# Even attention of a two-block transformer kernel: TensorE's order written out by steps of the heads

## The chip, the cores and the metric

The kernel runs on one core of one Trainium2 chip. A core has five engines that this text speaks of: TensorE (PE, matrix products, with its weight loads as PEld), VectorE (DVE), ScalarE (ACT), GpSimd (POOL) and SyncE (SP, which issues the loads). Each works through its own instructions in the order in which they stand; they wait for one another by semaphores. The metric is the device time of one execution in microseconds (us).

## The reference

Two blocks work on 512 tokens of 1024 features and on a context of 256 tokens. Block 0 ("even") mixes by a gated MLP over chunks and a differential attention; block 1 ("odd") by windowed attention; each is followed by a gated feed-forward part. The change lies in the even attention and the products beside it. Cut to that:

```python
u, v, q, k, vv = jnp.split(h @ w_in, [A_WIDTH, 2 * A_WIDTH, KV_START, KV_START + B_QK_WIDTH], axis=-1)
q = apply_rope(q.reshape(b, s_len, 2 * B_HEADS, HEAD_DIM), cos, sin)
k = apply_rope(k.reshape(b, s_len, 2 * B_HEADS, HEAD_DIM), cos, sin)
...
def diff_attn(q, k, v, lam):          # 4 heads, each a pair of 64-wide softmaxes
    s = jnp.einsum('bqhd,bkhd->bhqk', q, k).astype(jnp.float32) * ATTN_SCALE
    p = jax.nn.softmax(s, axis=-1).reshape(b, B_HEADS, 2, tq, tk)
    a = p[:, :, 0] - lam * p[:, :, 1]
    return jnp.einsum('bhqk,bkhe->bqhe', a.astype(v.dtype), v)
...
def chunk_mlp(u, v, w_s, b_s):        # u and v through Gelu, v normalised over 128 features,
    ...                               # mixed by a 128x128 matrix per group, times u
y = jnp.concatenate([chunk_mlp(u, v, w_s, b_s), diff_out(o, subln_g, lam_init)], axis=-1) @ w_out
```

`diff_out` is an RMS norm over a head's 128 features. The context goes through the same mixer with its own queries and keys.

## The kernel before

All activations lie transposed, features on the 128 partitions and the 768 tokens (512 and 256 of context) along the row. Products are taken in three passes with operands split into a high and a low part (`mm3`, lines 103 to 108: high x high, high x low, low x high). `split` (L122, L123) makes the parts: a cast on ScalarE, a subtraction on VectorE. Weights come by `blocks` and `unit`: a load, a cast on ScalarE (L81), a subtraction on GpSimd (L84).

In `even`, after the values are there (tiles `vhi`, `vlo`), three things are done side by side up to the output projection:

- The attention. There are four heads `t`, each with three pairs `qp` of blocks of 128 queries; pair 2 is the context's and sees 256 keys only. `stack_q` and `stack_k` lay a head's q and k out on the partitions as high and low halves (`qa`, `qb`, `kh`, `kl`). `softmax_diff` takes two score products (`c` = 0, 1) into `wide()` banks (tile `pw`, two of them), their maxima on VectorE (L538), their exponentials on ScalarE (L540, tile `e`), and the weighted difference on VectorE (L546). `attend` transposes the result in groups of four on TensorE (L558, into a `bank()`, tile `pb`, three of them), splits it (`ath`, `atl`) and multiplies by the values into `o`. `norm` squares `o`, sums on TensorE (L156), makes a reciprocal root in small VectorE instructions and spreads it (L183).
- Twelve filling products of 128 output features each, in a `fill()` bank (tile `pf`, a single one): four for q and k of heads 2 and 3 (`qk1`), eight for u and v (`gated`, tiles `raw`). Each is 24 instructions for the 512 tokens and 24 for the context, each followed by an evacuation on ScalarE (L445, L579).
- Gelu of the fillers (L626, another ScalarE table than Exp's), the transposes and statistics of the gate (`turn`, L638 to L643), and later its normalisation (L653, L655) and mixing (`mix`, L656).

What sets the order: the kernel is built with a scheduler that, per engine, takes the ready instruction of highest priority, and writes the order down; a chip follows that order. Heads 0 and 1 have a higher priority than the q/k fillers, heads 2 and 3 a higher one than the v fillers, and `issue_after` puts an instruction behind a named one in the scheduler's eyes. Heads 2 and 3 stand behind the last of the Gelus of the four v tiles:

```python
        for i in (4, 5, 6, 7):
            last = gelu(i, self.last_exp)
        with tc.high_priority(offset=tc.cur_priority - here), tc.issue_after(last.ins):
            head(2)
            head(3)
```

## Time and profile before

| what | us |
|---|---|
| median of 3 runs (1587.4 to 1593.12) | 1588.67 |
| the profiled execution, its own time | 1590.09 |
| its span in the profile | 1588.3 |
| TensorE busy, share of the span | 1517.7, 96% |
| VectorE busy | 1090.5, 69% |
| ScalarE busy | 723.5, 46% |
| GpSimd busy | 830.8, 52% |

The mean granted TensorE clock is 0.988 of full speed. A row of the order of time reads: start, duration, engine, line, operation, tile written <- tiles read, shapes, count; in brackets the idle time of the engine just before it and what ended that. "x4" merges four instructions that follow one another. The even attention and its fillers lie from about 129.5 us to 336 us, the output projection behind that.

### The profile page before, as it was taken

The page shows a single profiled execution, that of the slowest core. Times are in us where ns is not written, and L with a number is a line of the kernel's source. Part 1 is how long each engine was busy: PE and PEld are TensorE (multiplying, and loading weights), DVE is VectorE, ACT ScalarE, POOL GpSimd, SP SyncE. Part 2 cuts the span into 40 slices and gives each one's busy share as a digit, 9 for nine tenths or more (in the row PEclk, how much of TensorE's full clock was granted, in tenths as well). Part 3 has the DMA queues.
Part 4 walks back from the last instruction along what each step waited for, and adds up shares of the span by engine and source line. Part 5 has one row for each costly group of instructions (what it writes and reads, how often), then busy time and mean ns, then how long its engine had stood idle before and what let it go on. Part 6 is the DMA issues. An engine that isn't in the chain of part 4 may idle for free.

```text
span 1588.3 us, 24991 instructions
## 1 busy us (share of the span) xinstructions
PE 1517.7 (96%) x9547; PEld 1352.1 (85%) x9547; DVE 1090.5 (69%) x1958; ACT 723.5 (46%) x1472; POOL 830.8 (52%) x565
## 2 busy tenths in 40 slices
PE   6999997999999999999999989999999999999996
PEld 4767886889999999999999978777869989999996
DVE  3617847775697787888785485666667976666656
ACT  2415656553553333333333244565655644444443
POOL 0453321060347776777676415541304398888883
PEclk9999998999999999999999999999999999999998
DMA  9771010033223333444452122110225132323301
GB/s 353 290 253 60 28 33 1 1 133 133 67 74 120 113 109 118 139 163 141 162 169 63 27 66 67 60 34 12 70 80 206 54 120 87 113 91 109 93 14 54
DMA packets 54295, 162.00 MB, mean 102 GB/s; under 512 B 6176, under 2 KB 10656, under 8 KB 46496
## 3 DMA queue, kind: packets, MB, share of 16 engines
q1 hardware_dynamic: 47120, 135.11, 25.5%
q10 hardware_dynamic: 7056, 25.30, 4.9%
q8 instruction: 75, 1.23, 0.3%
q14 instruction: 44, 0.36, 0.1%
HBM read 158.29 MB, written 2.10 MB: 101 GB/s over the span
## 4 chain that ended last, share of the span: by engine, by line
PE 72%; DVE 8%; ACT 3%; issue 1%; POOL 0%; POOLq 0%; ACTq 0%; DVEq 0%
PE pw L108 10%; PE pw L106 10%; PE pw L107 10%; PE pb L108 8%; PE pb L107 8%; PE pb L106 8%; PE pf L106 3%; PE pf L107 3%; PE pf L108 3%; PE pb L1432 2%; PE pb L1421 2%; PE pw L1384 1%; PE pw L1392 1%; DVE t L884 1%; DVE T L123 1%
## 5 line engine op out<-in xcount | busy, mean ns | idle before, releaser
L84 POOL TENSOR_TENSOR w<-raw,w 128x512 fp32r<-128x512 f32 (+1 forms) x86 | 129.6, 1513 | 255.0 <-ACT w L81 232.7
L779 DVE SCALAR_TENSOR_TENSOR xT<-pb,mod,xT 128x512 f32<-128x512 f32 (+3 forms) x208 | 145.8, 707 | 125.9 <-PE pb L108 125.7
L106 PE MATMUL pw<-ax,w 128*128 128x384 f32 (+2 forms) x708 | 223.5, 319 | 4.1 <-DVE q L884 1.9
L107 PE MATMUL pw<-ax,w 128*128 128x384 f32 (+2 forms) x708 | 224.3, 318 | 2.7 <-DVE ax L465 1.4
L108 PE MATMUL pw<-ax,w 128*128 128x384 f32 (+2 forms) x708 | 223.7, 317 | 0.1
L884 POOL TENSOR_TENSOR w<-raw,w 128x512 fp32r<-128x512 f32 x110 | 169.0, 1552 | 19.7 <-ACT w L884 19.5
L884 POOL TENSOR_TENSOR w<-t,w 128x512 fp32r<-128x512 f32 x99 | 149.6, 1514 | 55.6 <-ACT w L884 55.6
L106 PE MATMUL pf<-ax,w 128*128 128x256 f32 (+2 forms) x484 | 163.2, 337 | 10.9 <-DVE qf L252 6.3
L106 PE MATMUL pb<-hh,w 128*128 128x512 f32 x480 | 171.0, 356 | 1.2 <-DVE xT L779 1.2
L108 PE MATMUL pb<-hh,w 128*128 128x512 f32 x480 | 171.5, 357 | 0.3 <-DVE w L884 0.3
L107 PE MATMUL pb<-hh,w 128*128 128x512 f32 x480 | 171.1, 356 | 0.0
L108 PE MATMUL pf<-ax,w 128*128 128x256 f32 (+2 forms) x484 | 161.1, 333 | 0.0
L107 PE MATMUL pf<-ax,w 128*128 128x256 f32 (+2 forms) x484 | 160.4, 331 | 0.0
L107 PE MATMUL pw<-T,w 128*128 128x384 f32 (+1 forms) x508 | 157.0, 310 | 1.2 <-DVE T L123 1.2
L106 PE MATMUL pw<-T,w 128*128 128x384 f32 (+1 forms) x508 | 156.3, 310 | 1.1 <-DVE hs L884 1.1
L108 PE MATMUL pw<-T,w 128*128 128x384 f32 (+1 forms) x508 | 157.0, 310 | 0.0
L106 PEld LDWEIGHTS pw<-ax,w 128*128 128x128 f32 x708 | 134.0, 190 | 9.7 <-DVE q L884 2.6
L107 PEld LDWEIGHTS pw<-ax,w 128*128 128x128 f32 x708 | 134.7, 190 | 8.4 <-DVE ax L201 2.4
L108 PEld LDWEIGHTS pw<-ax,w 128*128 128x128 f32 x708 | 134.6, 190 | 2.1 <-DVE w L953 0.4
L884 POOL TENSOR_TENSOR hh<-hs,hh 128x768 fp32r<-128x768 f32 (+1 forms) x42 | 80.2, 1910 | 90.1 <-ACT hh L884 67.6
L884 POOL TENSOR_TENSOR w<-rawo,w 128x512 fp32r<-128x512 f32 x59 | 103.6, 1756 | 28.3 <-ACT w L884 28.3
L106 PEld LDWEIGHTS pf<-ax,w 128*128 128x128 f32 x484 | 92.4, 191 | 19.6 <-DVE qf L252 3.8
(379 smaller groups left out, 3924.1 us busy)
## 6 DMA issues: line engine op xcount, KB each, us to landing
raw<-ffn_in SPq DMA_DIRECT2D x44, 1024.0 KB, 5.3
ar<-ada SPq DMA_DIRECT2D x24, 1024.0 KB, 7.1
ar<-ada ACTq DMA_DIRECT2D x48, 512.0 KB, 3.6
rawo<-ffn_out SPq DMA_DIRECT2D x88, 256.0 KB, 3.0
raw<-odd_out SPq DMA_DIRECT2D x32, 256.0 KB, 2.7
raw<-qk SPq DMA_DIRECT2D x16, 256.0 KB, 6.5
raw<-uv SPq DMA_DIRECT2D x16, 256.0 KB, 2.7
raw<-even_out SPq DMA_DIRECT2D x8, 512.0 KB, 3.6
```

What stands on the lines that cost most here:

```text
L84: eng.tensor_tensor(lo, raw, hi.bitcast(F32), ALU.subtract)
L106: mm(out, s[0], m[0], start=start, stop=False, **kw)
L107: mm(out, s[0], m[1], start=False, stop=False, **kw)
L108: return mm(out, s[1], m[0], start=False, stop=stop, **kw)
L123: return (lo_eng or nc.vector).tensor_tensor(lo, src, hi.bitcast(F32), ALU.subtract)
L779: ins = self.nc.vector.scalar_tensor_tensor(h, ps[:, r], self.modcol(l, j, m, who), h, ALU.mult, ALU.add)
L884: tail[key] = fn(*args, **kw)
L1384: nc.tensor.matmul(ps[:, st:en], Q, K[g][p][:, b0 * P:b1 * P], start=p == 0, stop=p == 1, skip_group_check=True)
L1392: nc.tensor.matmul(ps[:, en:en + TC], Q, K[g][p][:, TX:], start=p == 0 and not edge, stop=p == 1, skip_group_check=True)
L1421: last = nc.tensor.transpose(pt[:, x * P:(x + 1) * P], es[2 * (x % 2) + x // 2][:, kb * P:(kb + 1) * P], self.ident)
L1432: nc.tensor.matmul(po[64 * h:64 * h + 64, :], V[vb][:, 64 * g:64 * g + 64], t[:, h * TC:h * TC + TC], start=kb == 0, stop=kb == nb - 1, sk ...
```

## The change

The heads' functions are cut into steps, and every TensorE instruction of this part is put behind the one before it (`pe`, `tail`), so TensorE's order is the one written. There are 13 steps: step `n` does the scores of pair `n` and, in between, the transposes and value products of pair `n - 1`, by one of two plans. After each item `fill_in` takes pieces (six instructions: two of the eight k blocks) from one queue of all fillers, so many that their estimated time keeps up with 1.5 times (later 1.15 times) that of the attention. `stack` is made per half of a head (`c`), each with its own tile, all subtractions on VectorE (head 3's were GpSimd's); the transposes of `turn` go to `bank()` and stand in steps 9 to 11; the four Gelus of the v tiles come at the end of step 8.

```diff
+        def pe(fn, *args):
+            with tc.issue_after(tail[0].ins) if tail else ExitStack():
+                tail[:] = [fn(*args)]
...
+        def stack(t, c):
+            X, Y = (slice(0, 64), slice(64, 128))[::(1, -1)[c]]
...
+            nc.scalar.copy(m[X], q[X])
...
+            nc.scalar.copy(kh[X], k[X])
+            nc.scalar.copy(kh[Y], k[X])
+            nc.vector.tensor_tensor(m[Y], q[X], m[X].bitcast(F32), ALU.subtract)
+            for Z in (X, Y):
+                nc.vector.tensor_tensor(kl[Z], k[X], kh[X].bitcast(F32), ALU.subtract)
...
+        def block(name, n, out, scale, done=None):
...
+            for c, A, us in ((slice(0, TX), axx, 1.38), (slice(TX, TA), axc, 0.72)):
+                box = []
+                def step(k0, c=c, A=A, box=box):
+                    if k0 == 0:
+                        box.append(self.fill()[:, :c.stop - c.start])
+                    pe(piece, box[0], A, k0)
+                    if k0 == KT - 2:
+                        nc.scalar.mul(u[:, c], box[0], scale)
+                        if done and c.start:
+                            done(u)
...
-        here = tc.cur_priority
-        for n, key in enumerate((2, 6, 3, 7)):
-            W = self.blocks(a["qk1"][n])
...
-        with tc.high_priority(offset=tc.cur_priority - here):
-            QK = {0: stack(0)}
-            for t in range(2):
-                head(t)
...
-        for g in range(4):
-            turn(g)
-            gated(g, after if g == 3 else None)
+        share = (1.5, 1.15)
...
+        def fill_in(us):
+            clock[0] += us * share[n > 8]
+            while queue and clock[1] < clock[0]:
+                f, d, fn = queue.pop(0)
+                ahead(f + 3)
+                fn()
+                clock[1] += d
+        ahead(2)
+        stack(0, 0)
+        stack(0, 1)
...
+            long = prev and prev["qp"] < 2
+            plan = "00 01 t0 t1 a0 t2 10 11 a1 a2" if long else "00 t0 a0 01 10 11"
+            for v in plan.split():
+                if v[0] in "ta":
+                    if prev:
+                        (turned if v[0] == "t" else weighed)(prev, int(v[1]))
+                        fill_in(0.35 if v[0] == "t" else 0.71)
+                elif cur:
+                    i, c = int(v[0]), int(v[1])
+                    with tc.issue_after(last_gelu.ins) if last_gelu else ExitStack():
+                        scores(t, 2 * qp + i, c, cur["b"][i])
+                    fill_in(0.7 if qp < 2 else 0.24)
...
+                if t and qp < 2:
+                    norm(t - 1, 1 + qp)
+                    fill_in(1.2 - 0.5 * qp)
+                if n == 8:
+                    while queue[0][0] < 8:
+                        fill_in(0.5)
+                    for i in (4, 5, 6, 7):
+                        last_gelu = gelu(i, self.last_exp)
+                    fill_in(3.0)
+                if n >= 9:
+                    for g in ((0, 1), (2,), (3,))[n - 9]:
+                        turn(g)
+            prev = cur
+        fill_in(3.0)
+        norm(3, 1)
+        fill_in(100.0)
+        norm(3, 2)
```

In a plan, "00" is a score product (block, `c`), "t0" a group of transposes, "a0" the product with the values. The order of the built programs at three places (a number behind a tile's name is its own; `ax` and `w` are activations and weights of a filler, `pw` a score bank).

TensorE behind the last product ahead of the attention, before: 21 rows of the first filler like the first three stand ahead of these.

```order
L106 MATMUL pf_1065<-ax_328,w_1061 128x512
L107 MATMUL pf_1065<-ax_329,w_1061 128x512
L108 MATMUL pf_1065<-ax_328,w_1061 128x512
L536 MATMUL pw_1348<-kh_1332,qa_1326 128x512
L537 MATMUL pw_1348<-kh_1332,qa_1326 128x256
L536 MATMUL pw_1348<-kl_1333,qa_1326 128x512
L537 MATMUL pw_1348<-kl_1333,qa_1326 128x256
L536 MATMUL pw_1356<-kh_1338,qb_1327 128x512
L537 MATMUL pw_1356<-kh_1338,qb_1327 128x256
```

TensorE at the same place, changed; `t_997` belongs to the product ahead.

```order
L371 MATMUL pb_996<-ident_103,t_997 128x128 x4
L559 MATMUL pw_1106<-kh_1088,qa_1086 128x512
L560 MATMUL pw_1106<-kh_1088,qa_1086 128x256
L559 MATMUL pw_1106<-kl_1089,qa_1086 128x512
L560 MATMUL pw_1106<-kl_1089,qa_1086 128x256
L106 MATMUL pf_1126<-ax_314,w_1068 128x512
L107 MATMUL pf_1126<-ax_315,w_1068 128x512
L108 MATMUL pf_1126<-ax_314,w_1068 128x512
L106 MATMUL pf_1126<-ax_316,w_1068 128x512
L107 MATMUL pf_1126<-ax_317,w_1068 128x512
L108 MATMUL pf_1126<-ax_316,w_1068 128x512
```

The filler's 512 tokens stood whole ahead of the first score product; now that product comes first and a piece of six stands between it and the next.

VectorE at the same place, before (`qa_1532` and `kl_1539` are head 1's, `f_160` the first filler):

```order
L265 TENSOR_TENSOR qb_1327<-f_56_330,qb_1327 64x768
L279 TENSOR_TENSOR kl_1333<-f_57_331,kh_1332 64x768 x2
L265 TENSOR_TENSOR qa_1532<-f_58_332,qa_1532 64x768
L279 TENSOR_TENSOR kl_1339<-f_57_331,kh_1338 64x768 x2
L279 TENSOR_TENSOR kl_1539<-f_59_333,kh_1538 64x768 x2
L538 TENSOR_REDUCE sa_1346<-pw_1348 128x1
L251 STREAM_SHUFFLE sh_1117<-f_160_1064 128x512
L538 TENSOR_REDUCE sa_1346<-pw_1356 128x1
```

VectorE changed (`qa_1348` and `kl_1351` are head 1's):

```order
L546 TENSOR_TENSOR kl_1089<-f_57_331,kh_1088 64x768 x2
L544 TENSOR_TENSOR qa_1095<-f_56_330,qa_1095 64x768
L544 TENSOR_TENSOR qa_1348<-f_58_332,qa_1348 64x768
L546 TENSOR_TENSOR kl_1098<-f_57_331,kh_1097 64x768 x2
L567 TENSOR_REDUCE sa_1111<-pw_1106 128x1
L546 TENSOR_TENSOR kl_1351<-f_59_333,kh_1350 64x768 x2
L567 TENSOR_REDUCE sa_1111<-pw_1133 128x1
L579 SCALAR_TENSOR_TENSOR sx_1104<-sa_1112 128x1
L575 RECIPROCAL sa_1141<-sa_1112 128x1
```

The first maximum (of `pw_1106`) moved ahead of head 1's `kl`; the second stands behind that.

ScalarE at the end of the attention, before (`o_2463` is head 3's, `pf_3070` and `pf_3096` the two parts of the last filler):

```order
L570 COPY o_2463<-pb_2726 128x256
L595 ACTIVATE sq_2743<-o_2463 128x768
L653 ACTIVATE f_357_1917<-f_357_1917,sf_3161,sf_3149 128x128 x3
L653 ACTIVATE f_364_1980<-f_364_1980,sf_3161,sf_3149 128x128 x3
L653 ACTIVATE f_371_2043<-f_371_2043,sf_3161,sf_3149 128x128 x3
L653 ACTIVATE f_378_2106<-f_378_2106,sf_3161,sf_3149 128x128 x3
L579 COPY f_585_3069<-pf_3070 128x512
L122 CAST ax_3227<-o_1344 128x768
```

ScalarE changed (`pf_2966` is the context's part of the last filler but one, `pf_3033` the first part of the last):

```order
L122 CAST ath_3000<-pb_2995 128x512
L616 COPY o_2505<-pb_3004 128x256
L657 ACTIVATE sq_3024<-o_2505 128x768
L703 ACTIVATE f_160_1058<-f_160_1058,sf_3161,sf_3149 128x128 x3
L703 ACTIVATE f_161_1059<-f_161_1059,sf_3161,sf_3149 128x128 x3
L703 ACTIVATE f_162_1060<-f_162_1060,sf_3161,sf_3149 128x128 x3
L703 ACTIVATE f_163_1061<-f_163_1061,sf_3161,sf_3149 128x128 x3
L641 ACTIVATE f_166_1064<-pf_2966 128x256
L674 ACTIVATE f_166_1064<-f_166_1064 128x768
L641 ACTIVATE f_167_1065<-pf_3033 128x512
```

The twelve normalisations stood ahead of the evacuation of the last filler's first part; now they stand ahead of that of the last part of the filler before it, with a Gelu behind.

More of the change, by code (lines that the diff above doesn't have):

```diff
@@ L562, in attend @@
-                self.split(th, tl, pt)
+                        ins = nc.tensor.transpose(pt[:, j * TC + b * P:j * TC + (b + 1) * P],
+                                                  pair["b"][b]["e"][0][:, (2 * i + j) * P:(2 * i + j + 1) * P], self.ident)
+                return ins
+            pe(products)
+            th = Ra.tile([P, 512], F32R, name=self.uid("ath"), tag="at", bufs=6)
+            tl = Ra.tile([P, 512], F32R, name=self.uid("atl"), tag="at", bufs=6)
+            self.split(th, tl, pt)
@@ L635, in turn @@
             for off, n in halves:
[L636 to L638 removed]
+                ps = self.bank()
+                with tc.issue_after(tail[0].ins):
+                    for i in range(n):
+                        ins = nc.tensor.transpose(ps[:, i * P:(i + 1) * P], vg[:, (off + i) * P:(off + i + 1) * P], self.ident)
+                tail[:] = [ins]
                 nc.scalar.copy(vg[:, off * P:(off + n) * P], ps[:, :n * P])
@@ new lines, in even, with ahead @@
+        fillers = [block("qk1", n, (key, qk), 0.125 if key < 4 else 1.0, turn_em) for n, key in enumerate((2, 6, 3, 7))]
+        fillers += [block("uv", i, (i, raw), 1.0) for i in (4, 5, 6, 7, 0, 1, 2, 3)]
+        loads = [f[0] for f in fillers]
+        queue = [(n, us, fn) for n, f in enumerate(fillers) for us, fn in f[1]]
+        clock = [0.0, 0.0]
+        share = (1.5, 1.15)
+        def ahead(n):
+            while loads and len(fillers) - len(loads) < n:
+                loads.pop(0)()
```

170 lines of the change are left out of this document (86 added, 84 removed).

## The prediction

> **What bounds the kernel now.** I read the page first (busy shares, chain), then the stretches of the even attention, then the rows of its holes.
>
> ```profile
> span 1588.3 us, 24991 instructions
> PE 1517.7 (96%) x9547; PEld 1352.1 (85%) x9547; DVE 1090.5 (69%) x1958; ACT 723.5 (46%) x1472; POOL 830.8 (52%) x565
> PE 72%; DVE 8%; ACT 3%; issue 1%; POOL 0%; POOLq 0%; ACTq 0%; DVEq 0%
> ```
>
> TensorE (PE) is the bound: the kernel can only gain where TensorE stands still, and loses wherever it is made to. Columns of the next view: stretch, its length, busy time (instructions) of PE, weight loads, VectorE (DVE), ScalarE (ACT), GpSimd (POOL), then TensorE's granted clock, DMA share and GB/s.
>
> ```profile
> 130.00:155.00 25.00, 23.28 (x131) 19.80 (x131) 23.16 (x33) 15.35 (x26) 10.68 (x8) 1.00 0.11 33
> 155.00:190.00 35.00, 32.95 (x205) 29.02 (x204) 30.01 (x53) 21.90 (x45) 12.55 (x9) 1.00 0.15 46
> 190.00:235.00 45.00, 43.67 (x276) 38.72 (x275) 25.15 (x57) 25.27 (x49) 8.72 (x6) 1.00 0.10 30
> 235.00:260.00 25.00, 17.40 (x77) 13.80 (x76) 13.50 (x33) 13.82 (x25) 4.35 (x3) 0.73 0.00 1
> 260.00:330.00 70.00, 64.15 (x416) 55.45 (x415) 54.76 (x187) 42.65 (x93) 4.80 (x4) 1.00 0.11 38
> sum 200.00, PE 181.45 PEld 156.79 DVE 146.57 ACT 118.98 POOL 41.10; mean PE 36.29 PEld 31.36 DVE 29.31 ACT 23.80 POOL 8.22
> ```
>
> These 200 us are what the change rewrites. TensorE idles 200 - 181.45 = 18.6 us in them. VectorE is busy 146.6 us, and in the first 25 us 93%: early on it is nearly a second bound. The one large hole:
>
> ```profile
> 234.53 0.39 PE L106 MATMUL pf<-ax,w 128*128 128x256 f32 x1 [0.89 <-ACT f L579]
> ...
> 241.69 0.50 PE L536 MATMUL pw<-kh,qa 128*128 128x512 f32 x1 [2.91 <-ACT e L540]
> ...
> 247.06 0.47 PE L558 MATMUL pb<-ident,e 128*128 128x128 f32 x1 [2.87 <-DVE e L546]
> ...
> 253.75 0.63 PE L107 MATMUL pf<-ax,w 128*128 128x512 f32 x1
> ...
> 257.00 0.39 PE L107 MATMUL pf<-ax,w 128*128 128x512 f32 x1
> ```
> ```profile
> 238.49 0.85 ACT L626 ACTIVATE f<-f 128x768 f32<-128x768 f32 x1
> 239.35 1.28 ACT L540 ACT_TABLE_LOAD   x1
> 240.64 0.90 ACT L540 ACTIVATE e<-pw,sa 128x768 f32<-128x768 f32 x1
> ```
>
> Four filler products had to be finished before their Gelus, the Gelus before the table goes back to Exp, and head 2 behind that; nothing was left to fill with. TensorE's clock fell to half: the same product took 0.63 us at 253.75 and 0.39 at 257.00. A mean clock of 0.73 over 25 us is 13.5 us at half rate, two thirds of it busy, so about 4.5 us lost. One gap more: a product's modelled end lies 0.16 us behind the next one's start (0.39 long, 0.23 apart, rows below), so each of some 24 gaps hides 0.16 us: 3.6. With a few waits too short to be listed, before loses 18.6 + 4.5 + 3.6 + 2 = 29 us here (27 to 30). The products are the same in both kernels, so the forecast is the loss of the new order against this 29.
>
> **The change, part by part.** I walk the new order row by row with durations of this profile. First its start.
>
> ```profile
> 129.50 0.48 PE L106 MATMUL pf<-ax,w 128*128 128x512 f32 x1
> 129.81 0.40 PE L107 MATMUL pf<-ax,w 128*128 128x512 f32 x1
> 130.04 0.39 PE L108 MATMUL pf<-ax,w 128*128 128x512 f32 x1
> ...
> 135.04 0.39 PE L536 MATMUL pw<-kh,qa 128*128 128x512 f32 x1
> ...
> 135.74 0.39 PE L536 MATMUL pw<-kh,qb 128*128 128x512 f32 x1
> ```
> ```profile
> 128.93 0.84 ACT L261 ACTIVATE qa<-f 64x768 fp32r<-64x768 f32 x1
> ...
> 130.66 0.83 ACT L276 CAST kh<-f 64x768 fp32r<-64x768 f32 x1
> ...
> 139.96 0.90 ACT L540 ACTIVATE e<-pw,sa 128x768 f32<-128x768 f32 x1 [0.25 <-DVE sa L538]
> ```
> ```profile
> 130.07 0.95 DVE L265 TENSOR_TENSOR qa<-f,qa 64x768 fp32r<-64x768 f32 x1
> ...
> 132.28 1.91 DVE L279 TENSOR_TENSOR kl<-f,kh 64x768 fp32r<-64x768 f32 x2
> ...
> 138.97 0.96 DVE L538 TENSOR_REDUCE sa<-pw 128x1 f32<-128x768 f32 x1
> ...
> 145.34 1.02 DVE L546 SCALAR_TENSOR_TENSOR e<-e,sa,e 128x768 f32<-128x768 f32 x1
> ...
> 148.91 0.74 DVE L251 STREAM_SHUFFLE sh<-f 128x512 f32<-128x512 f32 x1
> 149.68 0.69 DVE L252 TENSOR_TENSOR f<-f,cos 128x512 f32<-128x512 f32 x1
> ```
>
> A score product takes 135.74 - 135.04 = 0.70 us, a piece of a filler six times 0.23 = 1.4 us (0.7 for the context's 256 columns). *Step 0.* Before, TensorE fills from 129.50 while the stacks are made. Now its next row is the first score product: kh is there at 131.5, kl (VectorE: qa 0.95, kl 1.9) at 133.2, score done at 133.7; one piece, 135.0. The second score's kl stands on VectorE behind two qa's, one for the next head: 133.2 + 4 x 0.95 = 137.0, done 137.4; piece, 138.7. The third wants the bank of the first: maximum (0.96, behind that kl) 137.9, exponential (0.90) 138.9, done 139.7; piece. The fourth wants the second's bank, whose maximum stands behind the next head's kl (1.9): 140.7, exponential 141.6, done 142.5; piece, 143.8. That is 4 x 0.70 + 4 x 1.4 = 8.3 us of work in 14.3: **6.0 lost**. *Step 1.* The same queue delays two scores by 2.0 us; the first transposes need the sum of weights (1.02) that stands behind shuffle, rope product (0.74, 0.69) and two maxima: 151.4, when TensorE is there at 148.6; then the split of the transposes 0.75 late and an evacuation 0.75: **6.3 lost**. Together 12, where before idles 1.7 us up to 155 (25.00 - 23.28).
>
> ```profile
> 327.62 0.39 PE L106 MATMUL pf<-ax,w 128*128 128x256 f32 x1 [1.44 <-ACT f L579]
> ...
> 332.06 1.16 PE L656 MATMUL pf<-sguT,f 128*128 128x128 f32 x8
> ...
> 336.14 0.42 PE L106 MATMUL pw<-ax,w 128*128 128x384 f32 x1
> ```
>
> *Steps 2 and 3*, walked alike: the stacks of two heads (six VectorE instructions of 0.95) stand ahead of a maximum: 2.6; the rest 1.1: **3.7**. *Steps 4 to 8.* All fillers share one PSUM bank. In three places the order puts a new tile's first piece right behind the old tile's last: the wait is 0.89 (row above, ScalarE free) to 1.44 (at 327.62, ScalarE busy), 1.15 taken as the middle: 3.5; three more are half covered, 1.5; weighed products too close behind their transposes, 0.9; VectorE and ScalarE queues 2: **8** (4 to 11).
>
> ```profile
> 309.98 0.59 ACT L122 CAST ath<-pb 128x512 fp32r<-128x512 f32 x1 [0.44 <-PE pb L558]
> ```
> ```profile
> 310.60 0.69 DVE L123 TENSOR_TENSOR atl<-pb,ath 128x512 fp32r<-128x512 f32 x1 [0.33 <-ACT ath L122]
> ```
>
> From a transpose group's start to its low half are 0.6 + 0.6 + 0.7 + 0.2 for hand-overs = 2.1 us; where the order puts less between, TensorE waits for the rest.
>
> *The Gelus (step 8).* Load 1.28 and three Gelus at 0.85 stand on ScalarE ahead of the evacuation that the next filler tile needs: 3.1; the second load ahead of nothing urgent; a split 0.9: **4.2**, against 13 in the hole. *Steps 9 to 11.* Four transpose groups of the gate want three banks, and their 12 statistics (with 12 aggregates) stand on VectorE ahead of the weights' splits: 3.5; others 2.3: **5.8**.
>
> ```profile
> 322.36 4.73 ACT L653 ACTIVATE f<-f,sf,sf 128x128 f32<-128x128 f32 x12 [2.01 <-DVE sf L704]
> 327.01 0.56 ACT L579 COPY f<-pf 128x512 f32<-128x512 f32 x1
> ```
> ```profile
> 319.39 0.18 DVE L135 TENSOR_SCALAR sf<-sf 128x24 int32<-128x24 int32 x1
> ...
> 321.71 0.18 DVE L139 SCALAR_TENSOR_TENSOR sf<-sf,sf 128x24 f32<-128x24 f32 x1
> ```
>
> *The last step.* A table load and two Gelus (3.0) stand ahead of a filler's evacuation: 2.3 after cover. The last transposes have nothing between them and their product: 2.2. Then ScalarE's order has the twelve normalisations (4.73 in one run, and behind VectorE's chain of small instructions, 321.71 + 0.18 - 319.39 = 2.5) ahead of the evacuation of the last but one filler, and TensorE's order has only that filler's next tile: TensorE done at 12.5 of this step, evacuation done at 17.8: **5.3**. Before pays 1.44 there, since the filler ahead of it was long. One more uncovered tile, 1.1. Sum **10.8**; the half clock may add 0 to 2.
>
> *The end.* From the last tile's start to the projection are 336.14 - 327.62 = 8.5 us; with the gate's normalisation done earlier it is four pieces of 0.7, about 1.4 of spread norms and 1.3 of gate products (1.16 for four in the row at 332.06, and two more), 5.5; less some 1 for the gate products now deferred: **2 gained**. GpSimd's stack of head 3 goes to VectorE (1.9 us, inside the walk). The loads of filler weights keep their order, two blocks ahead: nothing.
>
> Sum: 6.0 + 6.3 + 3.7 + 8 + 4.2 + 5.8 + 10.8 = 45 lost against 29, less 2: +14 us. The profiled execution's span is 1588.3; the runs' median is 1588.67, so 1588.7 + 14 = **1603 us** (0.9% slower).
>
> [...]
>
> **The rivals.** (a) *The same, 1588:* VectorE keeps nearer to TensorE than my walk has it (its rows overlap by some 0.08 us each, which I only partly count). Then steps 1 to 3 and 9 to 11 lose some 4 instead of 16, and 1603 - 12 = 1591, with the ends a little less 1588. For it: VectorE is busy 147 of 200 us only. Against: the first 25 us at 93%. It decides at the first transposes of step 1: a wait under 1 us is this case. (b) *Faster, 1574:* the pieces cover the chain of maximum, exponential and sum (about 4 us) everywhere after step 1, and only the start (6), the Gelus (4) and the last step (6) stay: 16 - 29 - 2 = -15. For it: 4 to 8 us of work lie between a step's last score and the transposes that need it. Against: single waits on one bank and on splits, which no sharing removes. It decides where steps 2 to 8 lose under 2 us in all. (c) *Slower still, 1608:* the clock halves at the start (busy under half in 129 to 139) and at the stall of 5.3, as it did behind the 2.91 us gap; a spell of 4 us at half rate costs 2 to 3, twice. [...]
>
> **How the numbers follow.** Main 0.41 (1596 to 1606), (c) 0.20, (a) 0.24, (b) 0.15. A difference under 0.5% (8 us) is about what this measurement can't tell from none, so faster 0.15, same 0.24, slower 0.61. The range leaves out (b) and the upper tail: 1581 to 1613; the likeliest case alone is 1596 to 1613.
>
> **What would show it.** Right: no half clock in the middle; TensorE waits at the first scores (5 to 6 us in all before 144); a wait of 2 to 3 us before step 1's transposes; one of about 5 us behind the last but one filler, released by ScalarE's evacuation; waits of fillers on their bank at ten places. Wrong: a sum of TensorE's idle time in the attention under 25 us, or an attention that ends before 331.

## The result, and the profile after

The changed kernel takes 1613.18 us (median of 5 runs, 1611.81 to 1617.22), the kernel before 1588.67 beside it (1587.4 to 1593.12): a ratio of 1.0153, 95% interval 1.0133 to 1.0173, or 24.5 us more. The prediction had 1603, with 1608 for its slowest rival, in which the clock halves. The profiled execution took 1613.23 us by its own time. The page:

```profile
span 1611.3 us, 24978 instructions
PE 1526.3 (95%) x9547; PEld 1358.2 (84%) x9547; DVE 1081.9 (67%) x1960; ACT 724.8 (45%) x1472; POOL 825.5 (51%) x563
```

TensorE has the same 9547 instructions and is busy 8.6 us longer with them. For the most part that is work at half the clock ("half rate" below). Where it lies shows in the stretches of the even attention (columns as before: stretch, length, busy time of PE, weight loads, DVE, ACT, POOL, then the granted clock, DMA share and GB/s):

```profile
129.00:147.80 18.80, 14.92 (x61) 11.61 (x61) 17.47 (x30) 12.15 (x21) 2.68 (x2) 0.82 0.05 15
147.80:174.00 26.20, 22.82 (x147) 20.24 (x148) 17.87 (x31) 14.98 (x31) 9.10 (x7) 1.00 0.13 41
174.00:183.00 9.00, 6.44 (x28) 5.22 (x27) 5.75 (x13) 4.45 (x9) 0.00 (x0) 0.81 0.00 0
183.00:219.00 36.00, 34.28 (x220) 30.26 (x219) 26.13 (x61) 17.68 (x37) 11.75 (x9) 1.00 0.10 30
219.00:230.40 11.40, 6.92 (x28) 5.84 (x28) 8.06 (x12) 6.37 (x13) 1.97 (x2) 0.70 0.14 46
230.40:272.00 41.60, 40.63 (x257) 35.58 (x256) 27.58 (x62) 22.31 (x47) 5.14 (x4) 1.00 0.06 20
272.00:282.00 10.00, 6.01 (x20) 4.65 (x18) 1.28 (x5) 5.80 (x9) 2.51 (x2) 0.66 0.00 0
282.00:324.90 42.90, 40.39 (x252) 34.72 (x250) 29.14 (x99) 23.02 (x48) 2.59 (x2) 1.00 0.00 1
324.90:343.10 18.20, 9.64 (x52) 8.00 (x52) 7.55 (x37) 10.78 (x24) 0.00 (x0) 0.81 0.44 145
343.10:355.30 12.20, 10.73 (x68) 9.01 (x67) 6.05 (x22) 6.01 (x8) 4.36 (x3) 1.00 0.00 0
sum 226.30, PE 192.78 PEld 165.11 DVE 146.88 ACT 123.55 POOL 40.10; mean PE 19.28 PEld 16.51 DVE 14.69 ACT 12.36 POOL 4.01
```

Before had one hole with a clock of 0.73. Now five stretches out of ten are below full clock, and each of them holds a wait of TensorE. The smallest clock that a short stretch shows is 0.50 (134 to 136), so a stretch's length times twice what its clock lacks of 1.00 is an estimate of its time at half rate: 6.8, 3.4, 6.8, 6.8 and 6.9 us. All waits together are 226.30 - 192.78 = 33.5 us. Grouped by what they waited for (total, times, longest):

```profile
PE pf L106 <- ACT f L641: 19.2, 10, 4.9
PE pb L588 <- DVE e L577: 3.8, 2, 2.6
PE pb L107 <- DVE atl L123: 3.1, 5, 1.3
```

Ten times TensorE stood at a filler's first product because ScalarE had not yet evacuated the one filler bank. Three of the ten (4.48, 3.98 and 4.91) make up 13.4 of the 19.2 us. The first of them, in ScalarE's and TensorE's order of time:

```profile
218.31 0.83 ACT L542 CAST kh<-f 64x768 fp32r<-64x768 f32 x1
...
222.91 0.83 ACT L543 CAST kh<-f 64x768 fp32r<-64x768 f32 x1
...
224.23 0.38 ACT L641 ACTIVATE f<-pf 128x256 f32<-128x256 f32 x1
```
```profile
219.89 0.28 PE L108 MATMUL pf<-ax,w 128*128 128x256 f32 x1
224.66 0.79 PE L106 MATMUL pf<-ax,w 128*128 128x512 f32 x1 [4.48 <-ACT f L641]
225.25 0.63 PE L107 MATMUL pf<-ax,w 128*128 128x512 f32 x1
...
230.85 0.39 PE L106 MATMUL pf<-ax,w 128*128 128x512 f32 x1
```

TensorE ends the filler's tile at 220.2. The evacuation that frees the bank starts at 224.23, behind the casts of two half heads (six of 0.83) and two exponentials. When TensorE goes on, a product of 128x512 takes 0.63 us and not 0.39, until 230.3. The second place is the Gelus (3.98 us at 272.5), the third the last step:

```profile
334.08 4.72 ACT L703 ACTIVATE f<-f,sf,sf 128x128 f32<-128x128 f32 x12 [0.72 <-DVE sf L798]
338.71 0.36 ACT L641 ACTIVATE f<-pf 128x256 f32<-128x256 f32 x1
```
```profile
339.12 0.80 PE L106 MATMUL pf<-ax,w 128*128 128x512 f32 x1 [4.91 <-ACT f L641]
...
343.33 0.39 PE L107 MATMUL pf<-ax,w 128*128 128x512 f32 x1
...
355.32 0.43 PE L106 MATMUL pw<-ax,w 128*128 128x384 f32 x1
```

At half rate such products follow one another by 0.43 us (rows from 225.25 to 227.38), else by 0.23 (from 230.61 on), so a spell at half rate loses 46% of its length. Part of each time at half rate still falls into the wait; counted from where TensorE goes on, the five spells are 5.7 us long (132.4 to 138.1), 3.5 (from 179.0), 5.7 (from 224.7), 5.0 (from 276.6) and 3.8 (from 339.1): 23.7 us, 10.9 lost. From its first weights' transpose (L371, at 128.33; before at 129.08) to the first product of the projection the attention takes 227.0 us, before 207.1.

### The profile page after: what moved, and what is told of

It reads as the page before. It is cut to its first block, busy times and chain, and to the rows that moved or that the text cites. A ratio compares the mean times of both kernels' runs of the same rounds, so it can differ in the third digit from the quotient of the medians.

```text
span 1611.3 us, 24978 instructions
## 1 busy us (share of the span) xinstructions
PE 1526.3 (95%) x9547; PEld 1358.2 (84%) x9547; DVE 1081.9 (67%) x1960; ACT 724.8 (45%) x1472; POOL 825.5 (51%) x563
## 3 DMA queue, kind: packets, MB, share of 16 engines
q8 instruction: 75, 1.23, 0.3%
## 4 chain that ended last, share of the span: by engine, by line
PE 78%; DVE 11%; issue 6%; ACT 3%; POOL 1%; DMA 1%; POOLq 0%; SPq 0%; DVEq 0%; ACTq 0%
PE pw L106 11%; PE pw L107 10%; PE pw L108 10%; PE pb L107 8%; PE pb L106 8%; PE pb L108 8%; PE pf L106 4%; PE pf L107 4%; PE pf L108 4%; PE pb L1526 2%; PE pb L1515 2%; PE pf L362 2%; PE pw L1478 1%; PE pw L1486 1%; DVE t L978 1%
## 5 line engine op out<-in xcount | busy, mean ns | idle before, releaser
L106 PE MATMUL pf<-ax,w 128*128 128x256 f32 (+2 forms) x484 | 167.7, 347 | 24.6 <-ACT f L641 19.2
L107 PE MATMUL pf<-ax,w 128*128 128x256 f32 (+2 forms) x484 | 163.1, 337 | 0.0
L108 PE MATMUL pf<-ax,w 128*128 128x256 f32 (+2 forms) x484 | 162.9, 337 | 0.0
```

The source lines that it names most:

```text
L106: mm(out, s[0], m[0], start=start, stop=False, **kw)
L107: mm(out, s[0], m[1], start=False, stop=False, **kw)
L108: return mm(out, s[1], m[0], start=False, stop=stop, **kw)
```

## The experiments

The theory (A) was: the order of ScalarE's queue ahead of the evacuations makes the long waits, and each wait leaves a spell at half rate behind it. The rivals: (B) the single filler bank is what counts, whatever ScalarE's order; (C) the work is only moved, and the next engine's queue makes the wait instead; (D) the half rate has another cause than the waits. Each run was compared with runs of the kernel before on the same chip; 0.1% is 1.6 us. "Attention" is the stretch from the transposes of L371 to the projection's first product, in the profiled execution.

| run | what differs from the changed kernel | ratio to before (95%) | attention, us |
|---|---|---|---|
| changed | | 1.0153 (1.0133 to 1.0173) | 227.0 |
| e_stack | casts of the stacks not ahead of time | 1.0124 (1.0104 to 1.0144) | 216.9 |
| e_gelu | Gelus behind the evacuation | 1.0128 (1.0102 to 1.0154) | 220.7 |
| e_norm | normalisations behind the evacuation | 1.0117 (1.0092 to 1.0143) | 220.1 |
| e_all | these three | 1.0078 (1.0055 to 1.0100) | 213.8 |
| e_spread | these, stacks placed by hand | 1.0086 (1.0070 to 1.0102) | 218.1 |
| e_start | as e_spread, two pieces ahead of the first score | 1.0125 (1.0109 to 1.0142) | 226.7 |
| e_dummy | as e_norm, products for nobody in two waits | 1.0081 (1.0066 to 1.0096) | 217.5 |
| e_bank | context tile of a filler in a rotating bank | 1.0035 (1.0021 to 1.0049) | 208.9 |
| e_bank_h | as e_bank, stacks of heads 2 and 3 not bunched | 1.0007 (0.9995 to 1.0020) | 203.4 |
| e_best | as e_bank_h, products for nobody at the start | 1.0033 (1.0017 to 1.0049) | 207.4 |
| e_best2 | as e_best, head 1's first half later | 1.0006 (0.9994 to 1.0019) | 204.4 |
| b_bank | the kernel BEFORE, with e_bank's edit | 1.0109 (1.0096 to 1.0123) | 219.4 |

A ratio and an attention time needn't agree: what lies ahead of the attention (128.0 to 130.6 us) and behind it (1252 to 1261 us) differs between these executions as well, also where no edit reaches. The profiled executions of e_bank and e_norm are the fastest of their runs (5.5 and 3.3 us under the median); that of e_best is 3.2 us above its median.

### ScalarE's order: e_stack, e_gelu, e_norm, e_all

`evac` holds the fillers' evacuations in the order written; `behind(x)` puts an instruction behind `x` in its engine's order.

```diff
 # e_stack, in stack()
-            nc.scalar.copy(m[X], q[X])
+            with behind(evac[-1] if evac else None):
+                nc.scalar.copy(m[X], q[X])
 ...     # and the same for the two copies into kh
 # e_gelu, at the end of step 8
+                    with behind(evac[-1]):
                         for i in (4, 5, 6, 7):
                             last_gelu = gelu(i, self.last_exp)
 # e_norm, in mix()
+                        with behind(evac[21]):
                             nc.scalar.activation(vg[:, s], vg[:, s], AF.Identity, ...)
```

> Undoes one thing: the three ScalarE casts of each half head may no longer run ahead; they stand behind the last filler evacuation written before them. TensorE's order in the attention stays. In the changed kernel TensorE waits 4.48 us (219.9 to 224.7) for an evacuation that stands behind six casts and two exponentials, and 2.56 (176.4 to 179.0) and 1.22 (147.8 to 149.0) for a sum of weights that stands on VectorE behind the subtractions of those casts; behind the first two its products run at half rate for 5.6 and 3.5 us, 2.6 and 1.6 us lost. As a side effect the scheduler here also puts the evacuation of the last but one filler ahead of the twelve normalisations (a wait of 4.91 us and 1.8 at half rate in the changed kernel). Theory A (ScalarE's order, and the half rate that follows each wait): all of these fall under 1 us each, 1613 - 3.9 - 2.4 - 1 - 4.2 = 1601.5, and less 6.3 for the side effect: about 1595. Rival B (the single filler bank, in whatever order ScalarE stands): the hand-over of the bank stays at 1 to 1.5 us each and the gain is the casts' part alone: 1606. Rival C (the work only moves: casts later make the next head's scores late): waits of 2 to 4 us appear ahead of the first or second score of steps 3, 6 and 9, and the time is 1606 to 1613.

> One thing alone: the table load and the four Gelus stand behind the evacuation of the last filler tile that they need, where the changed kernel has the load and three of them ahead of it. There TensorE waits 3.98 us (272.5 to 276.6) for that evacuation and then runs at half rate for 5.1 us (2.3 lost). Theory A: the wait falls to 0.5 to 1, no half rate there: 1613 - 3.2 - 2.3 = 1607.5. Rival C: the Gelus and the load back end 1 to 1.5 us later, the exponentials of the next step stand behind them, and TensorE waits there instead: 1611 or more, with a new wait of over 1 us between 284 and 292. In neither is anything changed before 268 or behind 295, so the other spells at half rate stay.

> One thing alone: the gate's twelve normalisations on ScalarE stand behind the evacuation of the last but one filler. In the changed kernel TensorE waits 4.91 us there (334.2 to 339.1) and runs at half rate for 3.9 us more (1.8 lost). Theory A: the wait falls under 0.5, no half rate: 1613 - 4.5 - 1.8 = 1606.5. Rival C: the normalisations end 0.4 us later, the last filler's evacuation stands behind them, TensorE waits there (0.69 us in the changed kernel) and the gate products come late: 2 to 3 us of the gain are given back, 1609. Rival D (the half rate at 339 has to do with something else than the wait, for example with the DMA burst in 333 to 343): the products behind it still take 0.63 us, 1608.5.

> All three together. Theory A: the parts add, since they lie 40 us and more apart: waits on the filler bank 19.2 -> about 5 us, half rate at the start alone (133 to 138), 1613 - 7.3 - 4.2 - 5.5 - 6.3 = 1590: level with the kernel before. Rivals B and C: 1600 or more, with ten hand-overs of the filler bank still at 1 us and more.

Measured against the changed kernel's 1.0153: the Gelus -0.25% (4 us, 5.5 expected), the normalisations -0.36% (5.7 us, 6.3 expected), the stacks -0.29% (4.6 us, 18 expected), all three -0.75% (12 us, 23 expected). The intervals leave the single differences barely clear of nothing, and that of the Gelus not clear; only the three together are plain. The single ones rest on the rows. The two places, first of e_gelu, then of e_norm:

```profile
275.03 0.50 PE L106 MATMUL pf<-ax,w 128*128 128x512 f32 x1 [0.47 <-ACT f L650]
275.37 0.39 PE L107 MATMUL pf<-ax,w 128*128 128x512 f32 x1
```
```profile
334.38 0.50 PE L106 MATMUL pf<-ax,w 128*128 128x512 f32 x1 [0.47 <-ACT f L650]
```

Both waits fell to 0.47 us, and no half rate stands directly behind them (granted clock 1.00 in e_gelu from 274 to 282, in e_norm from 334.3 to 343): theory A holds there. Rival C's new wait in 284 to 292 did not come. That nothing else would change did not hold: in e_gelu the wait at the normalisations fell too (4.91 to 3.07), and half rate came at a new place (clock 0.74 from 320 to 333), behind a wait of 1.95 us that the changed kernel has at full clock.

The stacks went rival C's way, though at another place than it named. The evacuation at 224 came in time, the 2.56 us at 179 were gone, and the side effect on the normalisations came too (0.47 us there), with a shorter wait at the Gelus (2.27 for 3.98); but the casts and subtractions of head 1's first half, which the changed kernel makes at the very start, now fell into the last step of head 0. From e_stack, VectorE and then TensorE:

```profile
172.72 2.88 DVE L557 TENSOR_TENSOR kl<-f,kh 64x768 fp32r<-64x768 f32 x2
175.63 1.11 DVE L590 SCALAR_TENSOR_TENSOR sx<-sa 128x1 f32<-128x1 f32 x1
176.66 0.68 DVE L123 TENSOR_TENSOR atl<-pb,ath 128x512 fp32r<-128x512 f32 x1
```
```profile
177.39 0.58 PE L107 MATMUL pb<-atl,vhi 128*128 128x256 f32 x1 [4.51 <-DVE atl L123]
```

The low half of the transposed weights (L123) stands behind the subtractions and a sum, and TensorE waits 4.51 us for it, more than the 2.56 that went. One further wait grew, 2.94 us for a split (1.31 in the changed kernel). The attention got 10.1 us shorter all the same; of that, 4.6 show in the time.

### Stacks placed by hand, and the start: e_spread, e_start

```diff
 # e_spread: the first half head of t + 1 behind "t2" of head t's last step, and VectorE's part behind the last split
+                        if v == "t2" and cur and qp == 2 and t < 3:
+                            stack(t + 1, 0)
 ...
+            with behind(lows[-1] if lows else None):
                 nc.vector.tensor_tensor(m[Y], q[X], m[X].bitcast(F32), ALU.subtract)
 # e_start: the same, and
         ahead(2)
+        fill_in(1.2)
         stack(0, 0)
```

> The three together, and the stacks of the next head placed by hand: the first half head stands behind the third group of transposes of a head's last step, the second at that step's end, the casts behind the last filler evacuation and VectorE's subtractions behind the last split of transposed weights. In the run of the three together TensorE waited 4.51 us (169.4 to 173.9) and 1.24 us for a split that stood behind three casts and the subtractions (kl 2.88 for two), and ran at half rate for 2 to 3 us behind it. Theory C2 (VectorE's and ScalarE's queues at the change of heads are the second bound: the stack must stand behind the splits): both waits under 1 us, 1602.7 - 4.5 - 1.2 = 1597. The 2.94 us at 152.6 stay, since no stack stands there. Rival (the queues are full there, in any order): the first or second score of steps 3, 6 and 9 waits 2 to 4 us for its low half instead, and the time stays at 1601 to 1604.

> The same, and one thing more: two pieces of the first filler stand ahead of the first score. At the start of the changed kernel TensorE waits 1.66 and 1.16 us for the first stack and then runs at half rate for 5.6 us (2.6 lost): prediction's step 0 put 6.0 there. If the start is a loss by itself: 2.8 + 2.6 less, about 5 under the run without it. Rival: the filler work is a fixed sum, two pieces spent here are missing where they cover something later, and the gain is under 2 us.

e_spread came out at 1.0086, no better than e_all (1.0078): its rival was right in the time, not in the place. The 4.51 us went and the 1.24 stayed (1.23 at 169.2, with half rate behind it); no score waits 2 us, but the transposes of the next head's first step now wait for their sums of weights, 1.79 us at 183.9 and 1.86 at 231.5 (L600 for L589), and half rate followed the second. With the fixed order each queue is full at a change of heads; moving one stack moves the wait.

e_start failed as an experiment on the start. The first waits fell as meant (1.66 and 1.16 to 0.31 and 0.60, with 1.27 for an exponential behind them), yet the run got slower, to 1.0125. Two pieces taken early shift every later piece against the steps, so that other work stands at each change of heads. At 184.8 a wait of 3.71 us for a split is new, and at 234.1:

```profile
234.12 0.90 PE L600 MATMUL pb<-ident,e 128*128 128x128 f32 x3 [4.12 <-DVE e L589]
```

e_spread has 1.86 us at the second place, and no wait for the split at the first. What the start costs by itself it can't tell; that a dealt order changes everywhere when one number changes, it shows.

### The half rate by itself: e_dummy

```diff
 # as e_norm, and in block(): fillers 5 and 8 begin with products that nobody reads
+                        more = {5: 19, 0: 17}.get(n, 0) if name == "uv" and not c.start else 0
+                        if more:
+                            pe(lambda pd: [nc.tensor.matmul(pd, vhi[0][:, :P], vhi[1], start=True, stop=True)
+                                           for _ in range(more)][-1], self.bank())
```

> Measures the half rate by itself. As the run with the normalisations alone (1609.5), and in the waits of 4.48 us (219.9 to 224.7) and 3.98 us (272.5 to 276.6) TensorE multiplies something nobody reads: 19 and 17 products of 128x512, 4.4 and 3.9 us. Nothing else of the work changes. If the half rate is what a wait leaves behind, the 5.6 and 5.1 us at half rate behind these two waits are gone (products of 128x512 at 0.39 us there, not 0.63) and the time falls by 2.6 + 2.3 to about 1604.5, though TensorE is not released a moment earlier. Rival (the rate falls there for another reason, such as what the other engines do): products behind the two places still take 0.63 us, and the time stays at 1609.5 or more.

At the first place, of e_norm and then of e_dummy:

```profile
224.69 0.80 PE L106 MATMUL pf<-ax,w 128*128 128x512 f32 x1 [4.49 <-ACT f L650]
...
225.71 0.63 PE L108 MATMUL pf<-ax,w 128*128 128x512 f32 x1
```
```profile
220.34 4.50 PE L649 MATMUL pb<-vhi,vhi 128*128 128x512 f32 x19
225.00 0.50 PE L106 MATMUL pf<-ax,w 128*128 128x512 f32 x1 [0.16 <-ACT f L654]
225.33 0.39 PE L107 MATMUL pf<-ax,w 128*128 128x512 f32 x1
```

TensorE is released at the same moment; only what it did meanwhile differs, and the products behind it take 0.39 and not 0.63 us. At the second place it is the same, and the granted clock is 1.00 at both (224 to 230 and 272 to 282). 1.0117 became 1.0081, 5.7 us against the 4.9 expected; the intervals overlap a little, and in the two profiled executions, where e_norm's is its fastest, the attention differs by 2.6 us only. So at these two places the half rate follows TensorE's standing still, and rival D falls there; the size is less sure than the cause.

### The bank: e_bank, e_bank_h, b_bank

```diff
 # e_bank, in block()
-                        box.append(self.fill()[:, :c.stop - c.start])
+                        box.append((self.bank if c.start else self.fill)()[:, :c.stop - c.start])
 # e_bank_h: the same, and for the first half of heads 2 and 3 the edit of e_stack
```

> The changed kernel with one thing else: the fillers' tile of the context (256 columns) lies in one of the three rotating banks, not in the filler's own, so that the next filler's first tile needn't wait for its evacuation. ScalarE's order is left as it is. Theory B (the single bank is the limit, not ScalarE's order): waits of fillers on the bank fall from 19.2 us to 6 or less, two or three spells at half rate go with them, and transposes and weighed products wait 2 to 4 us more for a bank: 1613 - 13 - 5 + 3 = 1598. Theory A (ScalarE's order is, in whichever bank the tile lies): the evacuations stay late, a rotating bank stays taken as long, transposes or weighed products wait there instead, and the time stays above 1606.

> The fillers' context tile in a rotating bank, and the first half heads of heads 2 and 3 no longer stacked early (their casts stand behind the last filler evacuation written before them). In the run with the bank alone (1597.8) the two longest waits left are 3.09 us (175 to 178) and 2.65 us (223 to 226), each for a sum of weights that stands on VectorE behind the subtractions of two half heads, 5.8 us in one piece, and TensorE runs at half rate behind each. Theory C2 (what is left is VectorE's order at the change of heads): with one half head ahead instead of two both waits fall under 0.5, 1597.8 - 5.2 - 3 = 1589.5. Rival (the queues are full in any order, as where the stacks were placed by hand): the same time to within 3 us, with new waits of 1 to 3 us for the splits in steps 4 and 7.

> The kernel before the change, with one thing else: its fillers' context tile also lies in a rotating bank. TensorE waited there for a filler's bank 2.3 us in all, of 18.6 idle; the hole of the Gelus (235 to 255) does not come from the bank. If the bank matters only where the order of the fillers is fixed by hand: 0 to 2 us less, 1589 to 1590.6. Rival: the scheduler uses the second bank to run fillers ahead, into the place of transposes: 1592 or more.

One line took back 1.0153 to 1.0035: 18.7 us, where 15 were expected. Rival B was right; that the median (1597.8) is its number (1598) is partly luck, since the kernel before took 1592.5 on that chip. ScalarE's order is as late as ever: the evacuation that ended the wait of 4.48 us starts 4.3 us behind its tile's last product (at 218.72) here too. But a late evacuation stops nobody when the next tile lies elsewhere. ScalarE's row, and TensorE's first product of the next tile, which doesn't wait:

```profile
223.06 0.38 ACT L641 ACTIVATE f<-pb 128x256 f32<-128x256 f32 x1
```
```profile
218.84 0.40 PE L106 MATMUL pf<-ax,w 128*128 128x512 f32 x1
```

The largest groups of TensorE's waits, two of e_bank and the first of e_bank_h:

```profile
PE pb L588 <- DVE e L577: 7.0, 3, 3.1
PE pb L107 <- DVE atl L123: 1.9, 5, 0.5
```
```profile
PE pb L107 <- DVE atl L123: 1.9, 5, 0.5
```

The 19.2 us on the filler bank are gone altogether. Of e_bank's 7.0 us two waits, 3.09 and 2.65, stood behind VectorE's subtractions of two half heads; with one at a time (e_bank_h) the group shrinks to 1.5 and the time is the kernel's before: 1.0007. Its attention, 203.4 us, is 3.7 shorter than before's, and what lies behind it gives that back (2.3 of it as told under "The end" below).

b_bank says what the bank was good for before. The same edit makes the kernel before 17 us slower, so the rival was right, and by far more than its "1592 or more" lets one think. In two stretches, first b_bank, then the kernel before:

```profile
125.00:160.00 35.00, 34.29 (x200) 28.57 (x200) 30.02 (x46) 22.18 (x39) 12.80 (x10) 1.00 0.15 46
...
265.00:335.00 70.00, 56.65 (x342) 48.55 (x341) 49.74 (x183) 37.12 (x82) 4.86 (x3) 0.90 0.07 25
```
```profile
125.00:160.00 35.00, 32.57 (x181) 26.16 (x180) 30.19 (x46) 22.40 (x39) 13.07 (x9) 1.00 0.14 42
...
265.00:335.00 70.00, 63.05 (x400) 53.39 (x398) 52.40 (x182) 42.68 (x89) 9.36 (x6) 1.00 0.11 38
```

Where the scheduler takes whatever is ready, a second bank lets the fillers run ahead: TensorE does 200 instructions ahead of 160 where it did 181. Counted in products of 512 columns (two of 256 for one), the fillers stand at 216 of 432 by 200 us, where they stood at 183; from 200 to 220 none follows, where 57 did, and from 300 to 320 none, where 40 did. In these parts TensorE stands (waits of 2.78, 3.89 and 3.17 us, at 211.6, 318.2 and 324.3) and half rate comes: 342 instructions for 400 from 265 to 335, with a clock of 0.90. The single bank had been holding the fillers back. Why the last of them wait until 320 stays open. In the order written by hand nothing can run ahead, and there the single bank only makes waits.

### The start, once more: e_best, e_best2

```diff
 # e_best: as e_bank_h, and ahead of the first score
+        def idle(n):
+            pe(lambda pd: [nc.tensor.matmul(pd, vhi[0][:, :P], vhi[1], start=True, stop=True) for _ in range(n)][-1], self.bank())
 ...
+        idle(12)
 # e_best2: the same, and the casts of head 1's first half behind evac[1]
```

> The same, and TensorE multiplies something nobody reads (12 products of 128x512, 2.8 us) ahead of the first score, in the wait for the first stack; no piece of a filler is moved, other than where two pieces stood there. If the start's half rate is left behind by the waits of 1.66 and 1.16 us: the products behind the first score take 0.39 and not 0.63 us, 2.6 us under the run without it, 1587. Rival (the busy share in 130 to 145 is low enough by itself, since each score waits for VectorE): the half rate comes 2 to 4 us later, and the time is the same to within 1 us.

> As the run with 12 products for nobody ahead of the first score, and the first half head of head 1 no longer stacked at the start: its casts stand behind the second filler evacuation (at about 154 us), where ScalarE and VectorE have been idle most of 5 us. In that run the second score waited 2.57 us for a low half that VectorE had put behind two qa's and a maximum, half rate came behind it, and transposes waited 1.57 and splits 3.06. If VectorE at the start is what is left (it was busy 93% of the first 25 us before): the 2.57 falls under 1, the 3.06 under 1.5, no half rate ahead of 145, and against the run without the 12 products (1592.3) 2.6 us of half rate and some 2.5 of waits are gone: 1587. Rival: the casts at 154 put the splits of step 1 off in their place, 2 to 3 us are lost there, and the time stays at 1592 or more.

e_best missed: 1.0033, worse than e_bank_h. No piece was moved, and the wait for the first stack was filled; but VectorE's order came out otherwise:

```profile
136.92 3.87 DVE L560 TENSOR_TENSOR kl<-f,kh 64x768 fp32r<-64x768 f32 x4
```
```profile
138.90 0.50 PE L573 MATMUL pw<-kl,qa 128*128 128x512 f32 x1 [2.57 <-DVE kl L560]
...
139.71 0.63 PE L107 MATMUL pf<-ax,w 128*128 128x512 f32 x1
```

A maximum now stands ahead of the second score's kl, behind head 1's qa that stood there before. TensorE waits 2.57 us there, and the half rate comes some 7 us later than in e_bank_h, from 139 on: the rival was right that it would only come later, and wrong that the time would be the same. In e_best2, with head 1 out of the way, that wait is 0.59 us and no product ahead of 145 runs at half rate; the 3.06 us for a split at 152 stayed, against the expectation, and half rate came behind that. 1.0006: the same as e_bank_h. So half rate early in the attention was moved twice and was never absent; what the start alone costs stays open. No run beat the kernel before; two are level with it.

## Why the prediction was right, and where its sizes were off

Right: slower; the mechanism (one filler bank, evacuated by a ScalarE that has other things ahead in its order); the ten waits of fillers on their bank, exactly ten; about 5 us behind the last but one filler, released by ScalarE's evacuation (4.91, forecast 5.3). Three of its signs failed: the waits ahead of 144 come to 2.8 us and not 5 to 6, the wait ahead of step 1's transposes is 1.22 us and not 2 to 3, and "no half clock in the middle" holds only for the old place of the hole (235 to 260 is at 1.00), since half rate came at 224.7 and, behind the Gelus, at 276.6.

The measured 1613.2 lies at the very end of the range on record (1581 to 1613), above the likeliest case (1596 to 1606) and above the slowest rival (1608). No case of the prediction gives such a time; that the range reaches it is luck. The forecast is wrong by 10 of 24.5 us, and by these terms of its sum (its additions are off by 0.1 to 0.2 us in places, 8.3 for 8.4 and 4.2 for 4.0, which changes nothing):

| term of the sum | forecast | measured |
|---|---|---|
| step 0, up to 143 | 6.0 | waits 2.8, half rate 2.6 |
| steps 1 to 3, up to 183 | 6.3 + 3.7 | waits 7.0, half rate 1.6 |
| steps 4 to 8 without the Gelus | 8 | waits 7.2, half rate 2.6 |
| Gelus | 4.2 | waits 4.0, half rate 2.3 |
| steps 9 to 11 | 5.8 | waits 2.5 |
| last step | 10.8 | waits 10.0, half rate 1.8 |
| half clock in all | 0 to 2 | 10.9 |
| the end and behind it | -2 | -2 + 2.2 + 1.6 |

- *The half clock* is the term that was mis-sized. The sum had "may add 0 to 2", for the last step alone; it came behind five waits and cost 10.9 us. That is rival (c), which had the right mechanism and named two of the five places, at 2 to 3 us each (measured 2.6 and 1.8). In the trace of before the half rate followed a gap of 2.91 us; in the changed kernel it also followed the 2.56 us and the start's 1.66 and 1.16. The spell of 4 us in (c) and the 0 to 2 of the sum rest on no run: they were the author's estimates. The spells at (c)'s two places came out 5.7 and 3.8 us long.
- *The waits* were over-sized: 5 to 6 us were named ahead of 144, and are 2.8 by their rows (the rest of step 0 is half rate); in all they are 33.5, where the walk had 45 with some 4 of hidden gaps in them. Most of that is in step 1 (1.22 us ahead of its first transposes, where 2 to 3 were named) and in steps 9 to 11 (2.5 for 5.8). Why is argued, not shown: the walk added up the delays of every queue, and where two engines are late at once only the later counts. This error and that of the half clock partly cancelled, which is luck too.
- *The long wait at 220 to 224.7* was in no term by its place: of its 8 us the sum put 5.0 on changes of the bank, the uncovered ones at 0.89 to 1.44 each. The size of the term was right (7.2) by luck: 4.5 of it is one wait, because the scheduler had brought a stack written two steps later ahead of the evacuation. That stands in the built program's order; the walk priced changes of the bank by before's rows.
- *The end.* From the last tile's start to the projection it is 6.6 us (348.75 to 355.32), 8.5 before: the 2 gained are there. But 8 of the gate's 48 instructions more lie behind the projection's start (1.1 us) and 0.9 of small waits with them:

```profile
L106 PE MATMUL pw<-T,w x508: 278/332/357, 448.3 to 1577.9; 128*128 128x384 f32 x86, 128*128 128x256 f32 x84
```
```profile
L106 PE MATMUL pw<-T,w x508: 278/332/356, 426.9 to 1554.7; 128*128 128x384 f32 x86, 128*128 128x256 f32 x84
```

The products of `T`, the next part's, start 93.0 us behind the projection's start (first row), 90.8 before (second row): 2.2 given back. Another 1.6 went further on, where a spell at half rate came in a part that the change doesn't touch (last section).

The rivals: (a), that VectorE keeps nearer, was to be told by the first transposes of step 1 with a wait under 1 us; it is 1.22, and steps 9 to 11 did go its way. (b) fell: steps 2 to 8 lost far more than 2 us. The sum priced the table load ahead of the Gelus at 1.28 us, and the rows show no more: the Gelu starts 0.01 us behind its load, and the load 0.02 us behind the instruction ahead of it, which ends at 271.88:

```profile
271.90 1.28 ACT L674 ACT_TABLE_LOAD   x1
273.19 0.84 ACT L674 ACTIVATE f<-f 128x768 f32<-128x768 f32 x1
```

## What to carry to other kernels

When an order is fixed by hand, give a tile that another engine must empty a second buffer, and look in the built order at what stands ahead of the emptying instruction on that engine; a scheduler's order may need the very same scarcity as a brake. As an estimate from this case, price a wait of TensorE of 2 us and more at its length and half again for the half rate that may follow (18.7 us of such waits in the changed kernel, the start's two counted as one, with 10.9 lost behind them). And after every edit read the order anew, since two pieces dealt earlier (e_start) moved waits of 4 us to places 50 and 100 us on.

## What the runs showed of the hardware that was not expected

The half rate doesn't follow a wait of a certain length every time. The wait for the bank of the last but one filler's second part, 1.94 to 1.96 us, left the clock at 1.00 in the changed kernel (320 to 334), e_stack (318 to 330) and e_all (318 to 328); in e_gelu, e_spread and e_dummy half rate came behind it (0.74 from 320 to 333, 0.83 from 320 to 330, 0.74 from 320 to 333). So it is with a wait of 1.90 us, some 940 us behind the projection's start, in a part with the same work; before and then after, 20 us around it:

```profile
1270.00:1290.00 20.00, 18.10 (x119) 16.29 (x118) 17.41 (x21) 9.12 (x19) 19.72 (x14) 1.00 0.35 105
```
```profile
1291.00:1311.00 20.00, 18.10 (x107) 16.21 (x106) 15.69 (x19) 8.52 (x18) 19.02 (x13) 0.91 0.32 94
```

Busy for 18.10 us in both, at full clock for 119 instructions in one and at 0.91 for 107 in the other. The time at half rate, worked out as above, is 3.6 us in this stretch, 3.4 or 6.8 to 6.9 in the five of the attention, and 13.5 in the one of before (25 us at 0.73): about one, two or four times the 3.4 of the stretch from 174 to 183 (9.00 us at 0.81). Why half rate follows one wait of 1.90 us and not the other is not shown. The half rate may be part of why a kernel's runs scatter: e_bank's ten lie between 1592.3 and 1602.4, at mean clocks of 0.984 to 0.989. It is not all, since runs of 1592.3 and 1598.7 both had 0.988.

A small instruction of VectorE stretched while GpSimd worked. In the changed kernel 22 of the 24 sums of 128x1 (L579) take 0.13 to 0.16 us, with no row of GpSimd beside them; the two that take 1.23 and 1.25 (from 148.87 and 189.87) have a subtraction of GpSimd beside them and end 0.02 us behind its end. In e_stack such a sum took 1.11 (175.63 to 176.74, row above), and GpSimd's subtraction beside it ends at 176.72:

```profile
174.75 1.97 POOL L84 TENSOR_TENSOR w<-raw,w 128x512 fp32r<-128x512 f32 x1
```

Again the two end 0.02 us apart; what holds the sum is not shown. Of the wait of 4.51 us some 1.9, by estimate, are VectorE's longer instructions: 2.88 for two subtractions that take 1.91 at 174.42 in the changed kernel, and 1.11 for 0.16. GpSimd's rows lie beside the two subtractions as well (172.94 to 176.72).
